# The head of a hybrid block: all tokens channels first, two blocks of u's product un-normed, the norm factor applied in the channel layout

## The chip, the cores and the metric

The kernel runs on one core of a Trainium2 chip. The metric is the device time of one execution in microseconds (us). The core has five engines that run side by side, each through its own instructions in order: TensorE (PE, with PEld for the loading of weights), VectorE (DVE), ScalarE (ACT), GpSimd (POOL) and SyncE (SP, which here only issues DMAs). An instruction waits until the engines and DMAs that make its inputs, or free its buffer, have signalled.

## The reference, cut to what matters

```python
def _mixer(xn, w_in, ...):
    proj = xn @ w_in                       # 1040 tokens x 1024 channels
    q, k, v, f_logit, u, gates = jnp.split(proj, SPLITS, axis=-1)
    y_a = _forgetting_attention(q, k, v, f_logit, b_forget) @ w_attn_out
    z = jax.nn.gelu(_s5(u, ...))           # 32 groups of 16 channels, 64 complex states each
    zg = z @ w_glu
    y_s = zg[..., :D_MODEL] * jax.nn.sigmoid(zg[..., D_MODEL:])
    g = jax.nn.sigmoid(gates)
    return (g[..., :D_MODEL] * y_a + g[..., D_MODEL:] * y_s) @ w_o

h = concatenate([meta, x])                 # 16 + 1024 tokens, 1024 channels
xn = _rmsnorm(h, norm_mix_g)               # h * rsqrt(mean(h*h) + eps) * g
h = h + _mixer(xn, ...)
h = h + _conv_ffn(_rmsnorm(h, norm_ffn_g), ...)
return _rmsnorm(h, norm_final_g)[N_META:]
```

Everything is float32. The norm factor of a token, `rsqrt(mean(h*h) + eps)`, is one number; a matrix product over channels may therefore be taken of `h * g` first and multiplied by the factor afterwards.

## The kernel before, in words

*Products.* A float32 operand is held as a pair, `hi` (rounded to what TensorE takes at speed) and `lo` (the rest), and each product is three matmuls: hi·hi, hi·lo, lo·hi. ACT makes `hi` by a cast, DVE makes `lo` by a subtraction (`split_lo`, L129).

*Layout.* TensorE contracts over the partitions, so the normed input is needed with channels on the partitions: the tiles `xhi` and `xlo`, 128 channels x 8 groups of channels x 1040 tokens. All projections read them.

*The head.* It makes `xhi` and `xlo` and computes u, 512 columns of the projection, in four blocks of tokens: block 0 has 272 (the 16 meta tokens and two tiles of 128), blocks 1 to 3 have 256 (two tiles each). A block's product is 4 groups of 128 columns (m = 0 to 3) x 8 groups of channels x 3 matmuls, 96 in all (`part`, L327 to L329).

- Block 0's tokens come channels first from DRAM (`x0t` into `xa`). ACT (L350) and DVE (L353) scale them by the norm's g and make the pair, without the norm factor. Their product enters four banks of PSUM (`first`) as the weights of u arrive. The factor is spread over the partitions: a DVE copy, a PE transpose (L370) and an ACT copy (L372) make `rsB`, and DVE multiplies the product by it on its way out of PSUM (L377).
- All other tokens, and block 0's once more, come as rows of 128 tokens (`xt`). ACT takes the sum of squares (L174), DVE and POOL make the factor (L176, L178: a power), DVE multiplies the rows by factor and g (L340), PE transposes them in eight pieces (L191), ACT and DVE make the pair (L193, L129). Block 0's tokens are made in this way last, behind block 3, since later products need them normed.
- ACT copies the products of blocks 1 to 3 out (L387). u is then written to DRAM by 32 DMAs (L394), those of m = 0 and 2 issued on SP, m = 1 and 3 on POOL, and is read back as `U` (L1724) in another layout for the SSM.

*Around the head.* The weights of the first gate columns are loaded behind the last row multiplication (L398, on POOL), cast by ACT (L399) and given their `lo` by ACT and an accumulating DMA (L135, L136). The SSM's tables are computed on DVE (L1456, L1459, with small copies on POOL, L1588 and L1589), and PE makes its kernel `Kt` (L1692) and its input map `Wi` (transposes L1713, copies on ACT L1714). The first SSM product is L1730, U with `Wi`. While these wait for data, PE works on the gate columns (L159 to L161). Later come q, k, v, the forget gate (L518, with weights `wf` made on POOL), the SSM's outputs, folded for a fast algorithm (`zf`, L559 on POOL; L584), attention, merge and the FFN.

*What sets the order.* A scheduler orders the instructions of each engine when the program is built, from a simulated timeline; `after(a, b)` adds an order by hand. The DMA loads of the head are chained on SP by `load` (L296), so that they arrive in the order written.

Of the kernel before, what the change touches and what calls it, by code (L numbers as in the profile page):

```python
# [9 lines left out]
F = mybir.dt.float32  # L10
# [3 lines left out]
AF = mybir.ActivationFunctionType  # L14
ALU = mybir.AluOpType
# [4 lines left out]
P = 128  # L20
# [27 lines left out]


@with_exitstack  # L50
def block_kernel(ctx, tc, x, meta, g1, x0t, g1t, w_q, w_k, w_v, w_f, w_u, w_g, b_f, w_ao, lam_d, bw_d, cw_d,
                 d_sk, l_dt, w_glu, w_o, g2, w_up, cwt_d, w_dn, gf, out, dbg=None, upto=99):
    nc = tc.nc
    dbg = dbg or {}
# [34 lines left out]
    def t_ps(name="tp"):  # L89
        return pp.tile([P, 512], F, tag="tp", name=name, bufs=2)  # L90
# [79 lines left out]
    def norm_factor(pl, src, n, bufs=10, sq=None):  # L170
        if sq is None:
            sq = pl.tile([P, D], BF, tag="sq", name="sq")
        ss = pl.tile([P, 1], F, tag="ss", name="ss", bufs=3)
        S.activation(sq[:n], src, AF.Square, accum_out=ss[:n])  # L174
        va = pl.tile([P, 1], F, tag="vr", name="vr", bufs=3)
        V.tensor_scalar(va[:n], ss[:n], 1.0 / D, EPS, ALU.mult, ALU.add)  # L176
        rs = pl.tile([P, 1], F, tag="rs", name="rs", bufs=bufs)
        GP.tensor_tensor(rs[:n], va[:n], nhalf[:n], ALU.pow)  # L178
        return rs
# [5 lines left out]
    def to_feature(xs, n, dhi, dlo, col, bank=st_ps):  # L185
        los = []
        for hf in range(2):
            tp = bank()
            t3 = tp.rearrange("p (k t) -> p k t", k=4)
            for k in range(4):  # L190
                PE.transpose(t3[:, k, :n], xs[:n, (4 * hf + k) * P:(4 * hf + k + 1) * P], ident[:n, :n])  # L191
            ho = dhi[:, 4 * hf:4 * hf + 4, col:col + n]
            S.copy(ho, t3[:, :, :n])  # L193
            los.append(split_lo(V, dlo[:, 4 * hf:4 * hf + 4, col:col + n], t3[:, :, :n], ho))
        return los
# [88 lines left out]
    uh = [wp.tile([P, 2, SW], R, tag=tag, name="uh") for tag in ("whi", "wlo") for _ in range(2)]  # L284
    xm = sp.tile([META, D], F, tag="tq", name="xm", bufs=3)

    xa = [sp.tile([P, 4, UN], F, tag="tq", name="xa", bufs=3) for _ in range(2)]
    g1T = n1.tile([P, KD], F, name="g1T")
    S.dma_start(g1T, g1t)
    S.dma_start(xm, meta)  # L290
    ssm_log, ssm_loads, ssm_steps = ssm(tc, after, sp, st_ps, ident, u_d, y_d, lam_d, bw_d, cw_d, d_sk, l_dt)
    queue = []

    def load(dst, src):

        queue.append(SY.dma_start(dst, src))  # L296
        if len(queue) > 1:
            after(*queue[:-3:-1])

    for j in range(4):  # L300
        load(xa[j // 2][:, 2 * (j % 2):2 * (j % 2) + 2], x0t[:, 2 * j:2 * j + 2])
        load(uraw[j], w_u[:, 2 * j:2 * j + 2])
    xts = [sp.tile([P, D], F, tag=tag, name="xt", bufs=n) for tag, n in (("Wi", 2), ("Gm", 2), ("sy", 3)) for _ in range(n)]
    g1B = xts.pop(4)
    g1_load = S.dma_start(g1B, g1.partition_broadcast(P))

    place = dict(zip((3, 4, 1, 2, 5, 6), xts))
    place[0] = xm

    def load_x(i):  # L310
        load(place[i], x[P * (i - 1):P * i])

    for i in range(1, 7):
# [11 lines left out]
    def part(ps, m, k, t, n):  # L325
        wh, wl = (w[k // 2][:, k % 2, P * m:P * m + P] for w in (uh, ul))
        PE.matmul(ps[:, :n], wh, xhi[:, k, t:t + n], start=(k == 0), stop=False)  # L327
        PE.matmul(ps[:, :n], wh, xlo[:, k, t:t + n], start=False, stop=False)
        PE.matmul(ps[:, :n], wl, xhi[:, k, t:t + n], start=False, stop=(k == KD - 1))  # L329

    def by_chunks(a):
        return a.rearrange("p (n j) -> p j n", j=CH)

    def factors(i):
        n = TILES[i][1]
        return norm_factor(n1, place[i][:n], n)

    def features(i, rs, behind=None):
        t, n = TILES[i]
        xn = V.scalar_tensor_tensor(out=place[i][:n], in0=place[i][:n], scalar=rs[:n], in1=g1B[:n],  # L340
                                    op0=ALU.mult, op1=ALU.mult)
        if behind is not None:
            after(xn, behind)
        return to_feature(place[i], n, xhi, xlo, t)[-1]

    first = [mm_ps() for _ in range(4)]
    for j in range(4):
        for k in (2 * j, 2 * j + 1):
            src, hi = xa[j // 2][:, k % 4], xhi[:, k, :UN]
            cp_ = S.activation(hi, src, AF.Copy, scale=g1T[:, k:k + 1])  # L350
            if k == 1:
                after(g1_load, cp_)
            V.scalar_tensor_tensor(out=xlo[:, k, :UN], in0=src, scalar=g1T[:, k:k + 1], in1=hi.bitcast(F),  # L353
                                   op0=ALU.mult, op1=ALU.subtract)
        S.copy(uh[j], uraw[j])
        split_lo(V, ul[j], uraw[j], uh[j])
        for m in range(4):
            for k in (2 * j, 2 * j + 1):
                part(first[m], m, k, 0, UN)
    for i in (7, 8):  # L360
        place[i] = sp.tile([P, D], F, tag="Tm", name="xt", bufs=2)
        load_x(i)

    rs0 = [factors(i) for i in range(3)]
    tp = t_ps()
    for i, rs in enumerate(rs0):
        t, n = TILES[i]
        rb = sp.tile([P, P], F, tag="wi", name="rb", bufs=2)
        V.tensor_copy(rb[:n], rs[:n].broadcast_to([n, P]))
        PE.transpose(tp[:, t:t + n], rb[:n], ident[:n, :n])  # L370
    rsB = sp.tile([P, UN], F, tag="wr", name="rsB", bufs=2)
    S.copy(rsB, tp[:, :UN])  # L372
    for i in (3, 4):
        ready = features(i, factors(i))
    n_log = len(ssm_log)
    for m in range(4):
        V.tensor_tensor(us[m][:, :, :UN // CH], by_chunks(first[m][:, :UN]), by_chunks(rsB), ALU.mult)  # L377

    for b, (t, n) in enumerate(UBLK[1:]):
        if b:  # L380
            for i in (3 + 2 * b, 4 + 2 * b):
                last = features(i, factors(i))
        for m in range(4):
            ps = mm_ps()
            for k in range(KD):
                part(ps, m, k, t, n)
            S.copy(us[m][:, :, t // CH:(t + n) // CH], by_chunks(ps[:, :n]))  # L387
# [1057 lines left out]
def ssm(tc, after, sp, s_ps, ident, u_d, y_d, lam_d, bw_d, cw_d, d_sk, l_dt):  # L1445
# [339 lines left out]
def _laid_out(x, meta_tokens, norm_mix_g, w_in, b_forget, w_attn_out, ssm_lambda_re, ssm_lambda_im, ssm_b_re, ssm_b_im,  # L1785
              ssm_c_re, ssm_c_im, ssm_d, ssm_log_dt, w_glu, w_o, norm_ffn_g, w_ffn_up, ffn_conv_w, ffn_conv_b,
              w_ffn_down, norm_final_g):
    import numpy as _np

    def by_rows(w):  # L1790

        return w.reshape(-1, P, w.shape[1]).transpose(1, 0, 2)

    def blocks(w):

        return w.reshape(w.shape[0] // P, P, -1, P).transpose(2, 1, 0, 3)
# [6 lines left out]
    x0 = _np.concatenate([meta_tokens, x[0]])[:UN]  # L1803
# [3 lines left out]
    return dict(x=x[0], meta=meta_tokens, g1=norm_mix_g[0], x0t=by_rows(x0.T), g1t=norm_mix_g[0].reshape(KD, P).T, w_q=blocks(q), w_k=blocks(k), w_v=by_rows(v),  # L1807
                w_f=by_rows(f), w_u=by_rows(u), w_g=blocks(g), b_f=b_forget[0], w_ao=blocks(w_attn_out[0]),
                lam=_np.concatenate([lam, lam]),
                bw=twice(ssm_b_re[0].transpose(1, 0, 2), ssm_b_im[0].transpose(1, 0, 2)),  # L1810
                cw=twice(ssm_c_re[0].transpose(2, 0, 1), ssm_c_im[0].transpose(2, 0, 1)),
                d_sk=ssm_d[0].reshape(G, GC).T, l_dt=ssm_log_dt[0], w_glu=blocks(w_glu[0]), w_o=w_o[0],
                g2=norm_ffn_g[0], w_up=blocks(w_ffn_up[0]), cwt=conv.reshape(4, -1, P).transpose(2, 0, 1),
                w_dn=w_ffn_down[0], gf=norm_final_g)
# [22 lines left out]
```

## Time and profile before

| what | value |
|---|---|
| time, median of 3 runs | 1486.72 us |
| lowest and highest run | 1483.04 and 1488.36 us |
| span of the profiled execution | 1485.7 us (the page gives no other time of it) |
| PE / PEld busy | 97% / 91% |
| DVE / ACT / POOL busy | 72% / 48% / 50% |
| mean DMA rate | 139 GB/s |

How to read the lines. A row of a stretch has its bounds and length in us, the busy time and count of PE, PEld, DVE, ACT and POOL, the clock granted to PE (1.00 is full), the DMA engines' busy share, and the GB/s. A row of a group has the line in the kernel, the engine, the operation, output and inputs, the shapes and the count; then the busy us, the mean ns of one, the idle time ahead and what ended it. A row of the timeline has start and length in us; in brackets stand the idle time ahead of it and what ended that. A row of waits has who waited for whom: us in total, times, the longest. SPq and POOLq are the queues on which DMAs are issued.

### The profile page before, as it was taken

How to read it: one execution, taken by the hardware profiler on the slowest of the kernel's cores; microseconds unless marked ns; L12 is line 12 of the kernel's file. 1: busy time of each engine (PE TensorE's matmuls, PEld its weight loads, DVE VectorE, ACT ScalarE, POOL GpSimd, SP SyncE). 2: the span in 40 equal slices, each digit the busy share in tenths (PEclk: the TensorE clock that was granted, in tenths of full speed). 3: DMA queues.
4: the chain of work that ended last, by engine and by line, in shares of the span. 5: the costliest groups of instructions: out<-in, count | busy, mean ns of one | idle time of the engine just before them, and what ended most of it. 6: DMA issues, size and time to landing. Idle time of an engine off the chain costs nothing. (4 is left out here: it accounts for less than half of the span.)

```text
span 1485.7 us, 26584 instructions
## 1 busy us (share of the span) xinstructions
PE 1440.4 (97%) x9712; PEld 1358.8 (91%) x9712; DVE 1071.4 (72%) x2173; ACT 712.2 (48%) x1384; POOL 742.1 (50%) x850
## 2 busy tenths in 40 slices
PE   7999997999999999999999999999999999998997
PEld 7989996998899999999888999999999999777886
DVE  6879648881566676647468987888877776788785
ACT  6434675541555665543546534444444445543433
POOL 1311125752456465524863144455544426789766
PEclk9999999999999999999999999999999999999999
DMA  6366571551127342047885135676653215765513
GB/s 246 86 157 157 128 163 50 177 160 43 48 79 178 93 111 90 26 148 256 257 158 185 57 109 141 178 199 188 174 143 100 84 57 180 286 203 148 168 40 114
DMA packets 91032, 206.72 MB, mean 139 GB/s; under 512 B 14651, under 2 KB 25531, under 8 KB 90517
## 3 DMA queue, kind: packets, MB, share of 16 engines
q1 hardware_dynamic: 69380, 159.73, 32.9%
q0 software_dynamic: 15296, 34.63, 13.2%
q10 hardware_dynamic: 6224, 10.65, 1.9%
q8 instruction: 77, 1.26, 0.3%
q14 instruction: 55, 0.44, 0.1%
HBM read 165.90 MB, written 69.35 MB: 158 GB/s over the span
## 5 line engine op out<-in xcount | busy, mean ns | idle before, releaser
L159 PE MATMUL mm<-xhi,whi 128*128 128x342 f32 (+2 forms) x488 | 159.4, 327 | 1.0 <-DVE q L129 1.0
L161 PE MATMUL mm<-xhi,wlo 128*128 128x342 f32 (+2 forms) x488 | 158.3, 325 | 0.0
L160 PE MATMUL mm<-xlo,whi 128*128 128x342 f32 (+2 forms) x488 | 157.7, 324 | 0.0
L1079 POOL TENSOR_TENSOR ov<-ov,og 128x1024 f32<-128x1024 f32 x21 | 51.1, 2434 | 125.6 <-ACT og L1078 121.7
L129 DVE TENSOR_TENSOR sw<-sf,sw 128x512 fp32r<-128x512 f32 x72 | 66.6, 925 | 50.0 <-ACT sw L1070 49.8
L1070 ACT CAST sw<-sf 128x512 fp32r<-128x512 f32 x72 | 44.9, 624 | 106.2 <-POOL sf L1196 74.5
L159 PEld LDWEIGHTS mm<-xhi,whi 128*128 128x128 f32 x488 | 91.9, 188 | 2.1 <-PE sp L714 0.8
L161 PEld LDWEIGHTS mm<-xhi,wlo 128*128 128x128 f32 x488 | 91.8, 188 | 0.3
L160 PEld LDWEIGHTS mm<-xlo,whi 128*128 128x128 f32 x488 | 91.9, 188 | 0.2
L763 ACT CAST th<-tp 128x256 fp32r<-128x256 f32 (+3 forms) x120 | 56.2, 472 | 62.5 <-PE tp L756 30.1
L129 DVE TENSOR_TENSOR tl<-tp,th 128x256 fp32r<-128x256 f32 (+3 forms) x120 | 65.2, 547 | 25.1 <-ACT th L763 23.7
L1196 POOL TENSOR_TENSOR sf<-raw,sf 128x512 f32<-128x512 f32 x36 | 59.1, 1641 | 44.8 <-DVE sw L129 44.7
L1196 POOL TENSOR_TENSOR sf<-raw 128x512 f32<-128x512 f32 x36 | 48.0, 1332 | 66.9 <-DMA raw<-in_w_up_dram 35.9
L221 PE MATMUL mm<-xhi,sw 128*128 128x258 f32 (+1 forms) x288 | 81.0, 281 | 0.0
L219 PE MATMUL mm<-xhi,sw 128*128 128x258 f32 (+1 forms) x288 | 80.8, 281 | 0.0
L220 PE MATMUL mm<-xlo,sw 128*128 128x258 f32 (+1 forms) x288 | 80.7, 280 | 0.0
L728 POOL TENSOR_SCALAR pt<-pt,nm 128x144 f32<-128x144 f32 (+4 forms) x72 | 51.8, 731 | 48.5 <-DVE nm L727 47.5
L1248 DVE SCALAR_TENSOR_TENSOR ov<-hv,cwt,ov 128x1024 f32<-128x1024 f32 x36 | 72.5, 2014 | 0.1
L1070 ACT CAST sw<-raw 128x512 fp32r<-128x512 f32 x70 | 43.0, 621 | 53.3 <-PE sp L221 25.5
L726 ACT ACTIVATE pt<-pt,nm 128x144 f32<-128x144 f32 (+4 forms) x72 | 52.9, 735 | 26.1 <-DVE nm L725 25.7
L719 DVE CUSTOM_DVE_ANT_0 pt<-sp,fb 128x328 f32<-128x328 f32 (+8 forms) x112 | 46.4, 430 | 20.0 <-PE sp L714 11.1
L756 PE MATMUL tp<-ident,pt 128*128 128x128 f32 (+1 forms) x360 | 58.3, 270 | 0.1
(708 smaller groups left out, 5702.1 us busy)
## 6 DMA issues: line engine op xcount, KB each, us to landing
raw<-in_w_up_dram SPq DMA_DIRECT2D x44, 512.0 KB, 3.6
t_d<-in_w_dn_dram POOLq DMA_DIRECT2D x44, 256.0 KB, 7.0
ar<-a_d SPq DMA_DIRECT2D x44, 256.0 KB, 5.1
wr<-t_d SPq DMA_DIRECT2D x44, 256.0 KB, 2.8
a_d<-ov SPq DMA_DIRECT2D x21, 512.0 KB, 2.6
wr<-in_w_dn_dram SPq DMA_DIRECT2D x33, 256.0 KB, 3.8
t_d<-in_w_dn_dram SPq DMA_DIRECT2D x22, 256.0 KB, 4.2
t_d<-t_d SPq DMA_DIRECT2D x22, 256.0 KB, 4.7
```

Of the source, the lines that this page charges most:

```text
L129: return eng.tensor_tensor(out_, src, hi.bitcast(F), ALU.subtract)
L159: yield PE.matmul(ps, whi[:, i, :], ahi[:, i], start=(i == 0), stop=False)
L160: yield PE.matmul(ps, whi[:, i, :], alo[:, i], start=False, stop=False)
L161: yield PE.matmul(ps, wlo[:, i, :], ahi[:, i], start=False, stop=(i == k - 1))
L219: PE.matmul(ps, a[0][:, i], bh, start=(i == 0 and not joins), stop=False, skip_group_check=True)
L220: PE.matmul(ps, a[0][:, i], bl, start=False, stop=False, skip_group_check=True)
L221: PE.matmul(ps, a[1][:, i], bh, start=False, stop=(i == kh - 1), skip_group_check=True)
L756: PE.transpose(tp[:kn, o:o + n], p_[:n, k0:k0 + kn], ident[:n, :n])
L763: S.copy(th[:kn, z:tw], tp[:kn, z:tw])
L1070: S.copy(hi, src)
L1196: sums.append(GP.tensor_tensor(f_, a, b, op))
L1248: V.scalar_tensor_tensor(out=o, in0=h_[:, j:SEQ + j], scalar=cwc(j, m), in1=o, op0=ALU.mult, op1=ALU.add)
```

## The change

The other tokens are loaded channels first as well (`xbt`, six more DMAs of 512 KB on SP); the rows are still loaded, but only for their sums of squares, and the row copy of g is no longer loaded. Block 1 enters u's product un-normed as block 0 does, and DVE multiplies its product by the factor on the way out. Block 0's product is copied out of PSUM by ACT, and POOL multiplies the copy by the factor afterwards. For every block the factor is spread over the partitions (`factors`). POOL then multiplies the channel tiles by it in place, and ACT and DVE make the normed pairs from them (`normed_features`): for blocks 2 and 3 ahead of their products, for blocks 0 and 1 for the later products. The transposes of the rows and the row multiplications go. Three small loads (the meta tokens, `l_dt`, `lam`) are issued on POOL's queue, not on ACT's.

In the order that the scheduler makes, POOL's queue has, one behind the other: the factors of the first tiles, block 0's four multiplications of u, block 0's channel tiles, block 1's, the remaining factors with the SSM's small copies, the issue of gate 0's load and of two more gate loads, then block 2's and block 3's channel tiles. ACT's queue has gate 0's cast ahead of the features of blocks 2 and 3. PE's queue has `Kt` ahead of the gate columns and 63 gate matmuls ahead of the first SSM product (before, some more). On SP, the second U is loaded behind the writes of `Tm` (before, right behind the first).

```diff
-    xa = [sp.tile([P, 4, UN], F, tag="tq", name="xa", bufs=3) for _ in range(2)]
+    xT = {0: [sp.tile([P, 4, UN], F, tag="tq", name="xa", bufs=3) for _ in range(2)]}
-    S.dma_start(xm, meta)
+    GP.dma_start(xm, meta)
...
-    g1_load = S.dma_start(g1B, g1.partition_broadcast(P))
...
+    def load_block(b, tag):
+        xT[b] = [sp.tile([P, 4, UBLK[b][1]], F, tag=tag, name="xT", bufs=2) for _ in range(2)]
+        for h_ in range(2):
+            load(xT[b][h_], xbt[b - 1, :, 4 * h_:4 * h_ + 4])
...
-    def features(i, rs, behind=None):
-        t, n = TILES[i]
-        xn = V.scalar_tensor_tensor(out=place[i][:n], in0=place[i][:n], scalar=rs[:n], in1=g1B[:n],
-                                    op0=ALU.mult, op1=ALU.mult)
-        if behind is not None:
-            after(xn, behind)
-        return to_feature(place[i], n, xhi, xlo, t)[-1]
+    def factors(b):
+        tp = t_ps()
+        t0, n_ = UBLK[b]
+        for i in TB[b]:
+            t, n = TILES[i]
+            rs = norm_factor(n1, place[i][:n], n)
+            rb = rbs[:n, i % 3]
+            V.tensor_copy(rb, rs[:n].broadcast_to([n, P]))
+            PE.transpose(tp[:, t - t0:t - t0 + n], rb, ident[:n, :n])
+        spread[b] = sp.tile([P, UN], F, tag=("wr", "wi")[b % 2], name="rsB", bufs=2)
+        S.copy(spread[b][:, :n_], tp[:, :n_])
+
+    def features(b, k):
+        t, n = UBLK[b]
+        src, hi = xT[b][k // 4][:, k % 4], xhi[:, k, t:t + n]
+        cp_ = S.activation(hi, src, AF.Copy, scale=g1T[:, k:k + 1])
+        cut = V.scalar_tensor_tensor(out=xlo[:, k, t:t + n], in0=src, scalar=g1T[:, k:k + 1], in1=hi.bitcast(F),
+                                     op0=ALU.mult, op1=ALU.subtract)
+        return cp_, cut
+
+    def normed_features(b):
+        t, n = UBLK[b]
+        for q in range(2):
+            GP.tensor_tensor(xT[b][q], xT[b][q], spread[b][:, :n].unsqueeze(1).broadcast_to([P, 4, n]), ALU.mult)
+        return [features(b, k)[1] for k in range(KD)][-1]
...
+    for m in range(4):
+        S.copy(us_part(0, m), by_chunks(first[m][:, :UN]))
+    ready = [features(1, k)[1] for k in range(KD)][-1]
+    factors(0)
     n_log = len(ssm_log)
+    factors(1)
     for m in range(4):
-        V.tensor_tensor(us[m][:, :, :UN // CH], by_chunks(first[m][:, :UN]), by_chunks(rsB), ALU.mult)
-    for b, (t, n) in enumerate(UBLK[1:]):
-        if b:
-            for i in (3 + 2 * b, 4 + 2 * b):
-                last = features(i, factors(i))
+        GP.tensor_tensor(us_part(0, m), us_part(0, m), by_chunks(spread[0]), ALU.mult)
+    for m in range(4):
+        ps = u_product(1, m)
+        V.tensor_tensor(us_part(1, m), by_chunks(ps[:, :UBLK[1][1]]), by_chunks(spread[1][:, :UBLK[1][1]]), ALU.mult)
+    for b in (2, 3):
+        factors(b)
+        normed_features(b)
+        if b == 3:
+            normed_features(0)
+            last = normed_features(1)
         for m in range(4):
-            ps = mm_ps()
-            for k in range(KD):
-                part(ps, m, k, t, n)
-            S.copy(us[m][:, :, t // CH:(t + n) // CH], by_chunks(ps[:, :n]))
-        if b == 2:
-            for i in range(3):
-                features(i, rs0[i], last)
+            ps = u_product(b, m)
+            S.copy(us_part(b, m), by_chunks(ps[:, :UBLK[b][1]]))
...
-    S.dma_start(ldt, l_dt.partition_broadcast(P))
+    GP.dma_start(ldt, l_dt.partition_broadcast(P))
-    S.dma_start(lam, lam_d)
+    GP.dma_start(lam, lam_d)
```

More of the change, by code (lines that the diff above doesn't have):

```diff
@@ L332, in by_chunks, with u_product, us_part @@
         return a.rearrange("p (n j) -> p j n", j=CH)
-    def factors(i):
-        n = TILES[i][1]
-        return norm_factor(n1, place[i][:n], n)
-    def features(i, rs, behind=None):
-        t, n = TILES[i]
-        xn = V.scalar_tensor_tensor(out=place[i][:n], in0=place[i][:n], scalar=rs[:n], in1=g1B[:n],
-                                    op0=ALU.mult, op1=ALU.mult)
-        if behind is not None:
-            after(xn, behind)
-        return to_feature(place[i], n, xhi, xlo, t)[-1]
+    TB = [(0, 1, 2), (3, 4), (5, 6), (7, 8)]
+    spread = {}
+    rbs = sp.tile([P, 3, P], F, tag="dt8", name="rb", bufs=1)
+    def factors(b):
[21 more added lines that the diff above has]
+        return [features(b, k)[1] for k in range(KD)][-1]
+    def u_product(b, m):
+        ps = mm_ps()
+        for k in range(KD):
+            part(ps, m, k, *UBLK[b])
+        return ps
+    def us_part(b, m):
+        t, n = UBLK[b]
+        return us[m][:, :, t // CH:(t + n) // CH]
     first = [mm_ps() for _ in range(4)]
@@ L348, in block_kernel @@
         for k in (2 * j, 2 * j + 1):
[L349 to L354, printed above, removed]
+            features(0, k)
         S.copy(uh[j], uraw[j])
@@ L359, in block_kernel @@
                 part(first[m], m, k, 0, UN)
+    load_block(2, "Tm")
+    for i in (5, 6):
+        load_x(i)
+    load_block(3, "Gm")
     for i in (7, 8):
-        place[i] = sp.tile([P, D], F, tag="Tm", name="xt", bufs=2)
         load_x(i)
[L364 to L374, printed above, removed]
+    for m in range(4):
+        S.copy(us_part(0, m), by_chunks(first[m][:, :UN]))
+    ready = [features(1, k)[1] for k in range(KD)][-1]
+    factors(0)
     n_log = len(ssm_log)
+    factors(1)
     for m in range(4):
-        V.tensor_tensor(us[m][:, :, :UN // CH], by_chunks(first[m][:, :UN]), by_chunks(rsB), ALU.mult)
-    for b, (t, n) in enumerate(UBLK[1:]):
-        if b:
-            for i in (3 + 2 * b, 4 + 2 * b):
-                last = features(i, factors(i))
-        for m in range(4):
-            ps = mm_ps()
-            for k in range(KD):
-                part(ps, m, k, t, n)
-            S.copy(us[m][:, :, t // CH:(t + n) // CH], by_chunks(ps[:, :n]))
-        if b == 2:
-            for i in range(3):
-                features(i, rs0[i], last)
+        GP.tensor_tensor(us_part(0, m), us_part(0, m), by_chunks(spread[0]), ALU.mult)
[8 more added lines that the diff above has]
+            last = normed_features(1)
+        for m in range(4):
+            ps = u_product(b, m)
+            S.copy(us_part(b, m), by_chunks(ps[:, :UBLK[b][1]]))
     for m in range(4):
@@ L1806, in _laid_out @@
     conv = _np.concatenate([ffn_conv_w[0], ffn_conv_b], axis=0)
[L1807 removed]
+    return dict(x=x[0], meta=meta_tokens, xbt=_np.stack([xT[:, :, t:t + n] for t, n in UBLK[1:]]),
+                x0t=xT[:, :, :UN], g1t=norm_mix_g[0].reshape(KD, P).T, w_q=blocks(q), w_k=blocks(k), w_v=by_rows(v),
                 w_f=by_rows(f), w_u=by_rows(u), w_g=blocks(g), b_f=b_forget[0], w_ao=blocks(w_attn_out[0]),
```

16 lines of the change are left out of this document (8 added, 8 removed).

## The prediction

> **What bounds the kernel now.** I read the page's busy shares and slices first, then the stretches of the head and of the stretch around 230 us, then PE's waits, then single rows. The page's own chain covers only the last instructions and says nothing of the head.
>
> ```profile
> span 1485.7 us, 26584 instructions
> PE 1440.4 (97%) x9712; PEld 1358.8 (91%) x9712; DVE 1071.4 (72%) x2173; ACT 712.2 (48%) x1384; POOL 742.1 (50%) x850
> PE   7999997999999999999999999999999999998997
> ```
>
> TensorE (PE) is busy 97% of the span; its first slice (37 us) is one of the few below 9. So whatever moves PE in the head moves the end, unless a later wait of PE takes it up. The stretches (PE, PEld, DVE, ACT, POOL busy, granted clock, DMA share, GB/s) and PE's waits up to 250 us:
>
> ```profile
> 20.00:25.00 5.00, 3.08 (x26) 2.84 (x25) 3.68 (x7) 3.48 (x8) 0.82 (x2) 1.00 1.02 410
> 30.00:35.00 5.00, 5.00 (x36) 5.00 (x35) 5.00 (x11) 1.18 (x2) 0.55 (x1) 0.77 0.01 2
> 92.80:100.00 7.20, 7.17 (x43) 6.81 (x44) 5.50 (x11) 4.45 (x12) 0.15 (x2) 0.76 0.27 76
> 220.00:230.00 10.00, 7.13 (x38) 6.78 (x38) 9.89 (x12) 6.31 (x11) 8.96 (x5) 0.84 0.05 19
> 230.00:240.00 10.00, 9.07 (x47) 7.18 (x45) 9.83 (x13) 5.76 (x13) 4.11 (x5) 0.82 0.18 52
> ```
> ```profile
> PE mm L518 <- POOL wf L129: 2.9, 1, 2.9
> PE sp L1730 <- ACT Wi L1714: 2.7, 1, 2.7
> ```
>
> PE waits in the head, is slowed after each wait (clock 0.77 and 0.76), waits once for U (L1730) and once for wf (L518, with the clock at 0.84 and 0.82 and DVE full beside it). POOL is nearly idle before 35 us.
>
> **The change, part by part.** Removed: 64 large PE transposes with their casts, and nine row multiplications on DVE.
>
> ```profile
> L191 PE MATMUL sp<-ident,xt 128*128 128x128 f32 x32 | 5.9, 314 | 4.8 <-DVE vr L176 3.1 <-DVE xlo L129 1.7
> L340 DVE SCALAR_TENSOR_TENSOR xt<-xt,rs 128x1024 f32<-128x1024 f32 x8 | 10.1, 1276 | 0.7 <-POOL rs L178 0.7
> L350 ACT ACTIVATE xhi<-xa,g1T 128x272 fp32r<-128x272 f32 x8 | 3.7, 512 | 1.1 <-DMA xa<-in_x0t_dram 1.0
> ```
>
> The sp half alone has 5.9 us of overlapping PE rows and 4.8 us of waits. DVE loses some 11.5 us of multiplications. In exchange ACT and DVE get 40 pairs like the third row, about 0.5 us each; they are spread over 60 us and each block's first pair is all that PE waits for, so I count 0.5 us a block. If that cover goes, a block's eight cost 4.
>
> Start and block 0. The meta tokens' square goes ahead of the first weight cast, a delay of 1.05; but the second pair of inputs comes by DMA anyway:
>
> ```profile
> 7.17 1.05 ACT L174 ACTIVATE sq<-xm 16x1024 bf16<-16x1024 f32 x1
> 11.12 0.93 ACT L350 ACTIVATE xhi<-xa,g1T 128x272 fp32r<-128x272 f32 x2 [1.04 <-DMA xa<-in_x0t_dram]
> 21.83 0.38 PE L370 MATMUL tp<-ident,rb 128*128 128x128 f32 x2
> 42.53 0.37 ACT L387 COPY usb<-po 128x256 f32<-128x256 f32 x1 [2.35 <-PE po L329]
> 67.94 0.28 PE L329 MATMUL po<-xhi,ul 128*128 128x256 f32 x1
> 68.65 0.28 PE L329 MATMUL po<-xhi,ul 128*128 128x256 f32 x1
> ```
>
> So block 0 ends near 22.3 instead of 21.83. Block 1 needs no norm now: the last two rows are two triples of matmuls apart, 0.355 a triple, so 32 triples are 11.36 and, with a few small transposes, block 1 ends near 34.1; before, its last copy came at 42.53. That is 8 us gained on PE.
>
> The loads: three more MB in channel layout, one of 0.5 MB gone; 2.5 MB at the 410 GB/s of the first stretch is 6.1 us more on SP's queue. They land by about 31, and POOL needs block 2's near 47, so nothing is charged. Were POOL quick, up to 6.1 would show. Three small DMAs move from ACT's queue to POOL's, idle there: nothing; at worst 1 us each on the SSM's tables.
>
> POOL is where the gain goes. It multiplies the copied u of block 0 (four of 128x8x34), block 0's channels (two of 128x1088), block 1's (two of 128x1024), and only then block 2's. The order of its queue puts those, the norm powers, the small SSM copies and the issue of gate 0's weights all ahead of block 2.
>
> ```profile
> L1079 POOL TENSOR_TENSOR ov<-ov,og 128x1024 f32<-128x1024 f32 x21 | 51.1, 2434 | 125.6 <-ACT og L1078 121.7 <-DVE ov L1109 3.9
> L600 POOL TENSOR_TENSOR cg<-cg,gl 128x342 f32<-128x342 f32 x24 | 22.8, 967 | 4.5 <-ACT cg L597 3.5 <-DMA gl<-g_d 1.0
> L559 POOL TENSOR_TENSOR zf<-zt 128x520 f32<-128x520 f32 x2 | 5.9, 2944 | 8.3 <-DMA zt<-y_d 8.3
> L178 POOL TENSOR_TENSOR rs<-vr,nhalf 128x1 f32<-128x1 f32 x8 | 5.3, 672 | 18.9 <-DVE vr L176 18.9
> 57.48 0.78 POOL L398 DMA_DIRECT2D g<-in_w_g_dram  x1
> 61.96 1.05 ACT L399 CAST g<-g 128x1024 fp32r<-128x1024 f32 x1 [4.81 <-DVE xt L340]
> 63.04 1.06 ACT L135 ACTIVATE g<-g 128x1024 fp32r<-128x1024 f32 x1
> 51.71 0.51 POOL L1588 COPY sm<-sm 128x32 f32<-128x32 f32 x3 [0.21 <-DVE sm L1456]
> ```
>
> Prices: 2.43 for 128x1024, in proportion 2.55 (estimate) for 1088. The u multiplication reads the factor with a stride of eight floats. Contiguous, two rows give (2434-967)/682 = 2.15 ns an element, hence 0.82 for 272; the strided row L559 gives 5.66 ns, hence 1.54. I take 1.5, because the stride is like L559's; ends 0.82 and 1.54. The Trainium skill, GPSIMD Engine Reference, section "7. Performance pitfalls for Q7 kernels", puts reads with a step above 8 bytes at half as much again, which speaks against this operand; by that rule the four would cost 1.23 each, an estimate, and the sum would be 1.1 lower. L559 is dearer than that rule.
>
> The powers of block 1 stand ahead in POOL's queue, and need ACT's squares behind the copies of block 0, so the u multiplications start near 25.4: block 0's end at 22.3, a copy of 0.37 and a square of 1.05 on ACT, a power of 0.67, and 1.0 for the hand-overs between engines (an estimate, after gaps such as the 0.7 of the L340 row). Then 4 x 1.5 = 6.0 to 31.4, 5.1 to 36.5, a power and 4.9 to 42.0, three powers (2.0) and fourteen small copies (2.4, by 0.51 for three) to 46.4. Here gate 0's load is issued. Its landing took 61.96 - 57.48 = 4.5, and ACT, in order, casts it (1.05 + 1.06) before it makes block 2's features: 46.4 + 4.5 + 2.0 = 52.9; POOL has block 2's first half by 50.7 (three DMA issues 1.9, one multiplication 2.4). With 0.5 for the first pair, PE starts block 2 at 53.4, 19.3 us after block 1. A wait brings the slow clock: at 0.77 over 5 us in the row above 1.2 is lost, more after a longer wait; I take 1.9 (ends 1.2 and 4). Blocks 2 and 3: 53.4 + 1.9 + 2 x 11.36 = 78.0.
>
> ```profile
> 73.53 0.58 PE L159 MATMUL mm<-xhi,g 128*128 128x342 f32 x2 [0.24 <-ACT xhi L193]
> 77.34 1.05 PE L1692 MATMUL sp<-Gm,sm 128*16 128x128 f32 x8
> 87.89 0.32 PE L159 MATMUL po<-xhi,whi 128*128 128x342 f32 x1
> 89.80 0.32 PE L159 MATMUL po<-xhi,whi 128*128 128x342 f32 x1
> 92.83 0.71 PE L1730 MATMUL sp<-U,Wi 128*128 128x130 f32 x4 [2.72 <-ACT Wi L1714]
> ```
>
> Before, PE went over to the gates at 73.53, after block 0's tokens were made again. After, nothing is left to be made: 78.0. **First term +4.5** (78.0 - 73.53; ends +1.1 with the cheap u price and the low clock loss, +8 with POOL a tenth dearer and the high one).
>
> U. Its data go out as writes of u, on SP one behind the other, and then come back:
>
> ```profile
> 64.01 0.63 ACT L387 COPY usb<-mm 128x256 f32<-128x256 f32 x2
> 64.39 14.65 SPq L394 DMA_DIRECT2D u_d<-usb  x16
> 79.14 1.18 SPq L1724 DMA_DIRECT2D U<-u_d  x2
> 92.19 0.59 ACT L1714 COPY Wi<-sp 128x512 f32<-128x512 f32 x1 [8.10 <-DMA U<-u_d]
> 80.00:84.00 4.00, 4.00 (x27) 4.00 (x26) 4.00 (x12) 1.89 (x3) 1.06 (x2) 1.00 1.08 217
> 88.00:92.00 4.00, 2.11 (x14) 1.83 (x12) 0.00 (x0) 0.00 (x0) 0.00 (x0) 1.00 1.04 312
> ```
>
> In the changed kernel the first column group of block 3 is done at 78.0 - 3 x 2.85 = 69.5, copied by 69.9; sixteen writes of 14.65 together end at 84.5, then U is issued. From issue to use it took 92.19 - 79.14 = 13.0; the second U went with it then and stands behind other loads now, which saves 0.5 MB at some 250 GB/s, 2.1. That is the late end, 95.4. The early end is 84.5 plus 0.5 MB at 410 GB/s, 1.3: 85.8. PE comes there at 78.0 + 1.9 (L1692) + 63 gate matmuls of 0.159 (twelve steps between the L159 rows are 1.91) + 0.9 = 90.8. So the wait is between 0 and 4.6 (7 with the second U's share put back). As much is on the DMA then as before, so I take 3.7, beside a clock loss like the old one of 0.24 x 7.2 = 1.7. **Second term: 3.7 - 2.7 = +1.0** (ends -4.4, no wait and no loss of clock, and +4.0).
>
> wf. In POOL's order it moves ahead of a multiplication and so comes earlier; its wait of 2.9 and some 2.9 of clock loss may go. But DVE stands at 9.89 and 9.83 of 10 there, so DVE's products are what is late next: only its 0.11 + 0.17 is left to gain. **Third term -0.3** (ends 0 and -5.8).
>
> Sum: 4.5 + 1.0 - 0.3 = +5.2 on a span of 1485.7. The profiled span is 1.0 below the median of the runs, 1486.7, and inside their spread, so I predict 1486.7 + 5.2 = 1491.9.
>
> **The rivals.** *U in time: no change.* U's wait is gone with its clock loss: 4.5 - 4.4 - 0.3 = -0.2, 1486.5. For it: U0 goes alone, and weights loaded at 58 to 64 before are fetched ten us ahead of the writes now. Against: a DMA share above 1 all through 80 to 92. It decides from a landing before 90.8.
>
> *Faster: wf decides.* The same with the wait at L518 and its slow clock really gone, which means that DVE's work there is not what PE needs next: 4.5 - 4.4 - 5.8 = -5.7, 1481.0; with POOL's contiguous price (2.7 less) 1478.3. It decides from 4.5 gained. For it: both stretches hold a clock of 0.82 to 0.84 and DVE comes lighter out of the head. Against: DVE full on both sides.
>
> *The change does nothing:* PE from 100 on absorbs any lateness in the waits near 230. Those waits hang on the same chain behind U, so I give it a part of the middle case alone.
>
> *By the clock rule.* The Trainium skill, TensorE: Matmul & The Clock Gate, section "What's actually happening", lets the clock fall only after some 3.4 us of idling; by that U's old wait of 2.7 should not have cost clock. The 0.76 row speaks against it. Had the loss another cause, it stays though U is in time: 4.5 - 2.7 - 0.3 = +1.5, 1488.2, still the middle case.
>
> **How the numbers follow.** No change, within 0.3% (4.5 us, about what this kernel's runs can tell): 0.30. Faster: 0.25. The forecast, slower: 0.45, own range 1488 to 1499. Two of ten left out at the ends of all cases: from 1480, just above the faster case's far end, to 1499 (+8 and +4.0 together are left out).
>
> **What would show it.** PE idle between about 34 and 53, released by ACT's features; POOL busy without a gap from 25; block 1's end near 34; gates from 78; a wait at the first product with U of some 3.7. Wrong if POOL's u multiplications take under 1 us, if block 2 begins before 48, or if PE gets U without waiting and the L518 wait is gone as well.

## The result, and the profile after

The changed kernel takes 1514.67 us (median of 4 runs, 1510.68 to 1515.74), the kernel before 1487.54 beside it: a ratio of 1.018, with a 95% interval of 1.0161 to 1.020. It is some 27 us slower, where 5.2 were predicted. The page of its profiled execution:

```profile
span 1513.8 us, 26522 instructions
PE 1434.2 (95%) x9646; PEld 1351.8 (89%) x9646; DVE 1091.4 (72%) x2192; ACT 721.1 (48%) x1409; POOL 765.6 (51%) x865
PE   6199998999999999999999999999999999998996
```

PE has 6.2 us less to do (1434.2 against 1440.4) and is idle for 79.6 us (1513.8 - 1434.2), against 45.3 before. The second slice shows where: 1 tenth busy. Up to the first product with U, PE is idle for 45.6 us (111.61 - 65.99), against 15.6 before (92.83 - 77.22); that is 30.0 of the 34.3. That stretch as a whole and two parts of it, first of the kernel before, then of the changed one:

```profile
0.00:92.83 92.83, 77.22 (x568) 74.64 (x568) 67.91 (x221) 42.01 (x75) 26.09 (x60) 0.96 0.61 182
40.00:60.00 20.00, 19.47 (x165) 19.03 (x164) 16.95 (x85) 5.19 (x12) 6.70 (x20) 1.00 0.05 10
60.00:80.00 20.00, 18.09 (x144) 16.89 (x143) 15.81 (x36) 10.71 (x19) 10.86 (x20) 1.00 0.88 220
```
```profile
0.00:111.61 111.61, 65.99 (x478) 63.48 (x479) 88.35 (x248) 50.99 (x100) 51.68 (x75) 0.83 0.54 170
40.00:60.00 20.00, 0.92 (x2) 0.36 (x2) 19.95 (x58) 3.33 (x9) 14.39 (x23) 0.50 0.23 79
60.00:80.00 20.00, 10.20 (x57) 9.53 (x58) 19.96 (x48) 9.13 (x20) 7.76 (x6) 0.59 0.17 27
```

Between 40 and 80 us PE does 11 us of work, partly at half clock; DVE (the third busy time) is busy without a gap, and POOL is not. PE's waits of the changed kernel up to 300 us, the longest but for the first weights, which both kernels wait for:

```profile
PE tp L351 <- DVE vr L176: 13.8, 1, 13.8
PE tp L351 <- DVE rb L350: 11.5, 2, 6.5
...
PE mm L332 <- DVE xlo L360: 6.6, 1, 6.6
PE mm L331 <- ACT xhi L359: 2.9, 1, 2.9
PE sp L1755 <- DMA U<-u_d: 2.7, 1, 2.7
```

Four of the five are in the head, 34.8 us together, and DVE ends 31.9 of these: PE's transposes that spread the norm factor (L351) wait for DVE's `vr` and `rb`, the products of block 2 (L332) for DVE's `lo` parts. Rows of PE, DVE, POOL and ACT in that stretch, with others between them left out:

```profile
33.82 0.28 PE L333 MATMUL po<-xhi,ul 128*128 128x256 f32 x1
63.87 1.01 PE L331 MATMUL mm<-xhi,uh 128*128 128x256 f32 x3 [2.89 <-ACT xhi L359]
71.68 0.58 PE L332 MATMUL mm<-xlo,uh 128*128 128x256 f32 x1 [6.59 <-DVE xlo L360]
111.61 0.68 PE L1755 MATMUL sp<-U,Wi 128*128 128x130 f32 x4 [2.73 <-DMA U<-u_d]
```
```profile
27.73 6.02 DVE L1478 TENSOR_SCALAR sm<-sm 128x32 f32<-128x32 f32 x1
54.33 5.42 DVE L360 SCALAR_TENSOR_TENSOR xlo<-xT,g1T,xhi 128x256 fp32r<-128x256 f32 x1
59.96 0.35 DVE L350 COPY rb<-rs 128x128 f32<-128x128 f32 x2
64.12 2.85 DVE L1481 TENSOR_TENSOR bt<-bw,sm 128x512 f32<-128x512 f32 x1
71.15 0.87 DVE L360 SCALAR_TENSOR_TENSOR xlo<-xT,g1T,xhi 128x256 fp32r<-128x256 f32 x2
```
```profile
25.00 3.69 POOL L403 TENSOR_TENSOR usb<-usb,rsB 128x272 f32<-128x272 f32 x4
28.66 5.04 POOL L367 TENSOR_TENSOR xa<-xa,rsB 128x1088 f32<-128x1088 f32 x2
36.61 0.59 POOL L178 TENSOR_TENSOR rs<-vr,nhalf 128x1 f32<-128x1 f32 x1 [2.90 <-DVE vr L176]
53.13 0.61 POOL L423 DMA_DIRECT2D g<-in_w_g_dram  x1 [1.35 <-DVE sm L1481]
54.80 4.65 POOL L367 TENSOR_TENSOR xT<-xT,rsB 128x1024 f32<-128x1024 f32 x2
61.46 4.96 POOL L367 TENSOR_TENSOR xT<-xT,rsB 128x1024 f32<-128x1024 f32 x2 [2.01 <-ACT rsB L353]
```
```profile
61.01 0.37 ACT L353 COPY rsB<-tp 128x256 f32<-128x256 f32 x1 [6.78 <-PE tp L351]
61.28 1.05 ACT L424 CAST g<-g 128x1024 fp32r<-128x1024 f32 x1
```

One operation of DVE on 128x32, 0.17 us long elsewhere, lasts 6.02 us: it starts with the last multiplication of u and ends as POOL's pair of multiplications on `xa` ends, at 33.7, so three POOL instructions went by. One `lo` operation lasts 5.42 and ends at 59.7, just behind POOL's pair on `xT`, at 59.5. One product of 128x512 lasts 2.85; it starts beside the last pair and ends 0.55 us behind it, at 66.97. The same two kinds of DVE operations over the whole stretch from 18 to 82 us, and that product, show how far they are lengthened: first the changed kernel, then one with the same instructions where the twelve large multiplications do not run on POOL (the first experiment below):

```profile
L360 DVE SCALAR_TENSOR_TENSOR xlo<-xT,g1T,xhi 128x256 fp32r<-128x256 f32 x28 | 17.2, 654 | 0.0
L1478 DVE TENSOR_SCALAR sm<-sm 128x32 f32<-128x32 f32 x20 | 9.8, 510 | 0.1
...
L1481 DVE TENSOR_TENSOR bt<-bw,sm 128x512 f32<-128x512 f32 x2 | 3.5, 1764 | 0.0
```
```profile
L360 DVE SCALAR_TENSOR_TENSOR xlo<-xT,g1T,xhi 128x256 fp32r<-128x256 f32 x28 | 12.1, 468 | 0.0
...
L1478 DVE TENSOR_SCALAR sm<-sm 128x32 f32<-128x32 f32 x20 | 3.1, 174 | 0.1
...
L1481 DVE TENSOR_TENSOR bt<-bw,sm 128x512 f32<-128x512 f32 x2 | 1.4, 682 | 0.0
```

In these three groups alone DVE is held for 13.9 us: 5.1 + 6.7 + 2.1. DVE then comes late to the factors and the `lo` parts, which stand behind the SSM's tables in its queue.

### The profile page after: what moved, and what is told of

It is laid out like the page before. It is cut to its first block, busy times and chain, and to the rows that moved or that the text cites. A ratio compares the mean times of both kernels' runs of the same rounds, so it can differ in the third digit from the quotient of the medians.

```text
span 1513.8 us, 26522 instructions
## 1 busy us (share of the span) xinstructions
PE 1434.2 (95%) x9646; PEld 1351.8 (89%) x9646; DVE 1091.4 (72%) x2192; ACT 721.1 (48%) x1409; POOL 765.6 (51%) x865
## 5 line engine op out<-in xcount | busy, mean ns | idle before, releaser
L129 DVE TENSOR_TENSOR sw<-sf,sw 128x512 fp32r<-128x512 f32 x72 | 71.1, 988 | 51.9 <-ACT sw L1095 51.9
L744 DVE CUSTOM_DVE_ANT_0 pt<-sp,fb 128x328 f32<-128x328 f32 (+8 forms) x112 | 46.4, 430 | 20.0 <-PE sp L739 11.8
L129 DVE TENSOR_TENSOR sw<-raw,sw 128x512 fp32r<-128x512 f32 x70 | 54.5, 782 | 5.9 <-ACT sw L1095 5.5
```

Source lines behind the costliest of these rows:

```text
L129: return eng.tensor_tensor(out_, src, hi.bitcast(F), ALU.subtract)
```

## The experiments

Three theories were set against each other. A is the prediction's: POOL's own queue holds block 2 back. B: DVE stands still while POOL multiplies. C: the order of DVE's queue, which has block 2's factors and `lo` parts behind the SSM's tables, does it. Ratios are to the kernel before on the same chip (medians of 1489.2 to 1490.6 there); the changed kernel stands at 1.018.

| run | edit | ratio, 95% interval |
|---|---|---|
| e1 | all twelve multiplications on DVE | 0.9961 (0.9946 to 0.9976) |
| e2 | channel multiplications cut thin | 1.0032 (1.0015 to 1.005) |
| e3 | SSM's tables later | 1.0028 (1.0015 to 1.0041) |
| e4 | blocks 0 and 1 last on POOL | 1.0148 (1.0132 to 1.0164) |
| e5 | before, with idle POOL work, two inputs | 1.0052 (1.0037 to 1.0067) |
| e6 | before, with idle POOL work, one input | 1.0069 (1.005 to 1.0088) |
| e7 | e1 and e3 together | 0.997 (0.9958 to 0.9983) |
| e8 | e7, and block 2 first on DVE | 1.0041 (1.0027 to 1.0055) |
| e9 | blocks 0 and 1 on DVE | 1.0099 (1.0076 to 1.0122) |
| e10 | blocks 2 and 3 on DVE | 1.0118 (1.0101 to 1.0135) |
| e11 | u's four on DVE | 1.0142 (1.0127 to 1.0157) |
| e12 | the three small loads back on ACT | 1.0175 (1.0156 to 1.0195) |

**e1, the multiplications on DVE.**

```diff
-            GP.tensor_tensor(xT[b][q], xT[b][q], spread[b][:, :n].unsqueeze(1).broadcast_to([P, 4, n]), ALU.mult)
+            V.tensor_tensor(xT[b][q], xT[b][q], spread[b][:, :n].unsqueeze(1).broadcast_to([P, 4, n]), ALU.mult)
...
-        GP.tensor_tensor(us_part(0, m), us_part(0, m), by_chunks(spread[0]), ALU.mult)
+        V.tensor_tensor(us_part(0, m), us_part(0, m), by_chunks(spread[0]), ALU.mult)
```

> The changed kernel, with its twelve large POOL multiplications (four of u, eight of channel tiles) issued on DVE instead. Theory A, POOL's own queue is what holds block 2 back (the prediction's mechanism): block 2 is released some 6 us earlier but DVE gets about 12 us more, so between no change and +6, 1514 to 1520 us. Theory B, DVE stands still while POOL multiplies (its rows between 25 and 67 us are about 21 us longer than the same rows elsewhere): DVE loses 21 and gains 12, so about 9 us or more faster, 1500 to 1506. Theory C, only the order of DVE's queue counts (factors and lo parts of block 2 behind the SSM's tables): 12 us more work in the same queue, 1522 to 1528.

1485.51 us: 33 us less than the changed kernel by the ratios ((1.018 - 0.9961) x 1489), and faster than the kernel before. That is more than B had said and the opposite of C. Of PE's 34.8 us of waits this one is left, and 1.5 for `xhi`:

```profile
PE tp L351 <- DVE rb L350: 9.4, 2, 5.1
```

DVE was given some 12 us of work (4 x 0.68 + 2 x 1.27 + 6 x 1.21) and lost its 14 and more of standing still, as the two fences of groups above show. The scheduler also put DVE's queue into another order here, so this run alone does not part B from C.

**e2, thin multiplications; e3, tables later; e4, blocks 0 and 1 late.** In e2 the output lacks the norm factor on all but 8 tokens of each block.

```diff
-            GP.tensor_tensor(xT[b][q], xT[b][q], spread[b][:, :n].unsqueeze(1).broadcast_to([P, 4, n]), ALU.mult)
+            GP.tensor_tensor(xT[b][q][:, :, :8], xT[b][q][:, :, :8], spread[b][:, :8].unsqueeze(1).broadcast_to([P, 4, 8]), ALU.mult)
```

> The changed kernel, with each of the eight POOL multiplications of channel tiles cut to 8 columns per channel group, so the norm factor is left out of the rest; all waits stay. Theory A: 19 us of POOL's queue go, block 2 no longer waits for POOL and is released about 6 us earlier by it, then by gate 0's cast: 1503 to 1508. Theory B: DVE loses some 17 fewer us to POOL, block 2's products start near 54 instead of 71.7: 1495 to 1499. Theory C: DVE's queue has the same work as before, so 1510 to 1514.

1494.49 us, 22 us less than the changed kernel, about as B had said. It is not as fast as e1, though it has less work: block 2 starts at 42.9, but then PE waits for U:

```profile
PE sp L1755 <- DMA U<-u_d: 6.2, 1, 6.2
```

In e3 a hand-written order holds the SSM's tables until block 2's normed pairs; POOL's work stays.

```diff
-        normed_features(b)
+        last_b = normed_features(b)
+        if b == 2:
+            ready = last_b
```

> The changed kernel, with one order by hand changed: the SSM's tables on DVE may start behind block 2's normed pairs, not behind block 1's un-normed ones. Theory A: no change, 1512 to 1516. Theory B alone: the same 21 us are lost on DVE, at another place; block 2's lo parts come some 10 us earlier, the tables as much later, 1504 to 1516. Theory C: block 2 starts near 55 instead of 71.7 and the SSM product waits for its tables instead, 1500 to 1508.

1493.26 us, 23 us less, and more than C had said; A had said no change. All twelve multiplications are still on POOL, and DVE is still held by them, but now at the places where it has little to do. POOL's multiplications of block 2 start at 46.18 instead of 54.80, though the same ones stand ahead of them: what has gone are POOL's waits for DVE and the small copies for the tables between them. A stretch and rows of POOL, DVE and PE:

```profile
20.00:40.00 20.00, 14.55 (x123) 14.34 (x121) 11.01 (x20) 13.85 (x33) 16.27 (x13) 0.91 0.70 257
```
```profile
46.18 9.27 POOL L367 TENSOR_TENSOR xT<-xT,rsB 128x1024 f32<-128x1024 f32 x4
```
```profile
32.34 5.36 DVE L360 SCALAR_TENSOR_TENSOR xlo<-xa,g1T,xhi 128x272 fp32r<-128x272 f32 x4
...
51.39 7.12 DVE L360 SCALAR_TENSOR_TENSOR xlo<-xT,g1T,xhi 128x256 fp32r<-128x256 f32 x8 [5.46 <-ACT xhi L359]
```
```profile
55.80 0.58 PE L332 MATMUL mm<-xlo,uh 128*128 128x256 f32 x1 [3.16 <-DVE xlo L360]
```

POOL is busy for 16.27 of these 20 us and DVE for 11.01, against 19.28 in the changed kernel; the eight `lo` parts of block 2 take 7.12 where eight free ones are 3.7 (468 ns each). PE has block 2 under way at 55.8, not at 71.7. Here and in most of the runs below the scheduler moved other instructions too, on POOL as well as on DVE.

In e4 the two blocks that PE needs last come last on POOL.

```diff
+            if behind is not None:
+                after(mu, behind)
...
-            normed_features(0)
-            last = normed_features(1)
+            normed_features(0, last3)
+            last = normed_features(1, last3)
```

> The changed kernel, with POOL's multiplications of blocks 0 and 1 ordered behind block 3's. Theory A: 9.7 us of multiplications leave POOL's queue ahead of block 2, so block 2 starts about 10 us earlier: 1501 to 1505. Theory B: DVE's 21 us of standing still move, about 10 of them behind block 2: 1503 to 1508. Theory C: block 2's factors still stand behind the tables in DVE's queue, less than 4 us gained: 1510 to 1515.

1513.18 us, 5 us less than the changed kernel by the ratios. POOL's queue was relieved of 9.7 us ahead of block 2, and block 2 did start early, at 44.4 instead of 63.87. A's 1501 to 1505 are missed all the same, because the time was lost again behind it. The holding went with the multiplications to where the `lo` parts of the later blocks stand, and PE waited for them. And gate 0's load, which waits for block 1's pairs, was issued at 99.21 instead of 53.13, so that PE waited for its cast as well:

```profile
L360 DVE SCALAR_TENSOR_TENSOR xlo<-xT,g1T,xhi 128x256 fp32r<-128x256 f32 x20 | 16.6, 902 | 3.1 <-ACT xhi L359 3.1
```
```profile
PE mm L332 <- DVE xlo L360: 8.0, 5, 2.2
PE mm L159 <- ACT g L426: 4.3, 1, 4.3
```

So this run does not decide against A by itself. e1 and e3 do: e1 came out 33 us faster where A had said none to 6 slower, and e3 gained 23 where A had said none.

**e5 and e6, idle POOL work in the kernel before.** Neither touches the norm or the loads of the kernel before; POOL only gets work that nobody needs. The order of DVE's queue in the head is that of before in e6 but for one row multiplication; in e5 some rows of tables and `lo` parts moved as well.

```diff
+    pad = uraw[0].rearrange("p a n -> p (a n)")
+    for _ in range(8):                                   # e5
+        after(GP.tensor_tensor(pad, pad, pad, ALU.mult), ready)
+    for _ in range(18):                                  # e6, in place of the eight
+        after(GP.tensor_scalar(pad, pad, 1.0, 0.0, ALU.mult, ALU.add), ready)
```

> The kernel before, with eight idle multiplications of 128x1024 by itself on POOL (two inputs, 19.5 us in all), between 25 and 55 us, where POOL has little to do and DVE is full; its output is unchanged. Theory A, only POOL's queue counts: the factors of the last tiles stand behind some of them, 0 to 4 us slower than before. Theory B, DVE stands still while POOL multiplies: DVE's rows in that stretch grow by 10 to 19 us in all, and the kernel is 5 to 12 us slower than before.

> The kernel before, with eighteen idle POOL operations of one input and a constant on 128x1024 (19.4 us in all) at the same place; its output is unchanged. Theory A: as the run with two inputs, 0 to 4 us slower than before. Theory B, if two tensor inputs are what holds DVE up: DVE's rows keep their length, 0 to 4 us slower, and at least 4 us faster than the run with two inputs. Theory B, if any large POOL operation holds DVE up: as the run with two inputs.

1497.99 and 1500.10 us: 0.52% and 0.69% slower, 8 and 10 us. PE waits for DVE's `lo` parts (L328) for 8.8 and 10.1 us, where it was 0.3 before. The work has one input or two, the loss is much the same, so it does not take two inputs on POOL. DVE and POOL rows of e6, then of e5:

```profile
37.51 1.02 DVE L1456 TENSOR_SCALAR sm<-sm 128x32 f32<-128x32 f32 x1
38.68 1.03 DVE L1456 TENSOR_SCALAR sm<-sm 128x32 int32<-128x32 f32 x1
```
```profile
35.33 11.30 POOL L377 TENSOR_SCALAR uraw<-uraw 128x1024 f32<-128x1024 f32 x9
```
```profile
37.95 1.27 DVE L340 SCALAR_TENSOR_TENSOR xt<-xt,rs 128x1024 f32<-128x1024 f32 x1
39.15 1.87 DVE L1456 TENSOR_SCALAR sm<-sm 128x32 f32<-128x32 f32 x1
```
```profile
36.04 9.94 POOL L377 TENSOR_TENSOR uraw<-uraw 128x1024 f32<-128x1024 f32 x4
```

A DVE operation of 0.17 us takes 1.02 beside POOL operations of 1.04 each, and 1.87 beside those of 1.89: it lasts until the POOL instruction beside it ends. Then one or two of DVE's get in before POOL's next: the 1.27 in e5 is the operation's own length, and POOL's four take 9.94 us, not 4 x 1.89 = 7.6. In these two runs the engines take turns by whole instructions; in the changed kernel, as shown above, one DVE instruction stood through two or three of POOL's. The idle work also stood ahead of two norm factors in POOL's own queue, and no run takes that part of the 8 to 10 us away; the lengths of DVE's rows do not depend on it.

**e7 and e8, the two cures together.** e7 has the edits of e1 and e3. e8 has besides the order of e4, with the multiplications on DVE.

> The changed kernel with both edits that were tried one by one: the twelve multiplications on DVE, and the SSM's tables behind block 2's normed pairs. If DVE's standing still and its order are two causes that add up: PE's remaining waits for the factors (9.4 us with the multiplications on DVE) shrink to some 4, 1478 to 1483 us. If they are one cause (with nothing standing still the order is harmless): as with the multiplications alone, 1484 to 1487; and if the tables then come late for the SSM's first product, slower than that, 1488 to 1494.

> As the run before, and besides the multiplications of blocks 0 and 1 ordered behind block 3's pairs, so that block 2 stands first in DVE's queue. If DVE's queue is what holds block 2 back: PE's idle time between block 1 and block 2 falls below 5 us, 1474 to 1480 us unless the SSM's tables or the normed blocks 0 and 1 come late for the gates. Theory A, POOL's queue: nothing of it is left there, as the multiplications on DVE alone, 1484 to 1487.

e7 takes 1485.69 us, as e1 does (their intervals overlap): the two gains of 33 and 23 us do not add up. Both act on the same lateness: DVE's queue is too long in front of block 2, because of what holds it and because of what stands in it. With the holding taken away the order no longer matters (e7 against e1); with the order changed the holding still costs some 8 us (1.0028 in e3 against 0.997 in e7). e8 takes 1496.63 and misses its expectation by 17 us. Block 2 does start early, at 38.3, but PE then waits for what was put behind it:

```profile
PE po L159 <- ACT whi L146: 10.6, 1, 10.6
...
PE sp L1742 <- DVE Vm L1485: 3.9, 2, 2.1
```

As in e4, the edit also moved gate 0's load: it was issued at 81.70, in e1 at 42.88. With the holding gone, neither change of order gained anything: e7 is as fast as e1, and e8 only has others wait.

**e9 to e12, the parts.** The channel multiplications of blocks 0 and 1 alone, those of blocks 2 and 3 alone, and those of u alone went to DVE; in e12 only the three small loads went back.

```diff
-            GP.tensor_tensor(xT[b][q], xT[b][q], ...
+            (V if b < 2 else GP).tensor_tensor(xT[b][q], xT[b][q], ...      # e9
+            (V if b > 1 else GP).tensor_tensor(xT[b][q], xT[b][q], ...      # e10
...
-        GP.tensor_tensor(us_part(0, m), us_part(0, m), ...
+        V.tensor_tensor(us_part(0, m), us_part(0, m), ...                   # e11
...
-    GP.dma_start(xm, meta)
+    S.dma_start(xm, meta)                                                   # e12, and l_dt and lam likewise
```

> The changed kernel with only the channel multiplications of blocks 0 and 1 on DVE (u's four, and blocks 2 and 3, stay on POOL). If DVE's standing still counts by its length: it loses some 10 us fewer between 28 and 42 us and gains 4.8 of work, so 4 to 8 us faster than the changed kernel, 1506 to 1510. If it counts only where block 2's factors and pairs are in the queue (54 to 67 us): no change, 1512 to 1516.

> The changed kernel with only the channel multiplications of blocks 2 and 3 on DVE, in nearly the same order of DVE's queue. If DVE's standing still counts by its length: it loses some 9 us fewer between 54 and 67 us and gains 4.7 of work, 4 to 8 us faster than the changed kernel, 1506 to 1510. If it counts only where block 2's pairs are in the queue: 8 to 14 us faster, 1500 to 1506, and most of the gain of all twelve is here. If the order is all: 3 to 5 us slower, 1517 to 1520.

> The changed kernel with only the four multiplications of u's block 0 on DVE. They took 3.7 us on POOL and held DVE for about 1.5; on DVE they are 2.5 us of work: no change, 1512 to 1517. The prediction's price for them, 1.5 us each on POOL, was too high, and if they were what POOL's queue turned on, 3 to 4 us faster, 1510.

> The changed kernel with the three small loads (meta tokens, l_dt, lam) back on ACT's queue. By the prediction's price of nothing: 1512 to 1517. If the tables' start hangs on them, up to 3 us either way.

e9: 1502.77 us, e10: 1506.68, e11: 1510.71. By the ratios that is 12, 9 and 6 us less than the changed kernel, 27 together of e1's 33, each with some 4 us either way: every part of the holding costs something, and none of them carries it all. That holds for this order of DVE's queue; e3 shows that where the holding falls matters too. e10 is the cleanest of these runs for B: DVE's queue is that of the changed kernel up to the first multiplication that was moved, and it gets 4.7 us more work. Still it is faster, with the held `lo` parts back at their length and block 2 starting without the wait of 6.59. Behind that multiplication some `lo` parts now stand ahead of the last tables, and what this is worth was not tried:

```profile
L360 DVE SCALAR_TENSOR_TENSOR xlo<-xT,g1T,xhi 128x256 fp32r<-128x256 f32 x29 | 12.9, 478 | 0.0
```
```profile
57.32 1.01 PE L331 MATMUL mm<-xhi,uh 128*128 128x256 f32 x3 [3.01 <-ACT xhi L359]
```

e9 and e11 were better than expected; in both the scheduler moved DVE's queue as well, and how much of their 12 and 6 us is order was not tried. e12, 1.0175 against 1.018, is no change.

## Why the prediction was wrong

Its direction was right; its size was not, and neither was its reason.

- *Start, block 0, block 1.* Right. The last matmul of block 1 ends at 34.1 (33.82 + 0.28), the predicted 34.1.
- *Loads, small loads.* Right: nothing in PE's waits ends with them, and e12 is no change.
- *POOL's prices.* The channel multiplications were right (5.04 and 4.65 a pair, predicted 5.1 and 4.9). u's were 0.92 each, not 1.5: the strided row L559 was the wrong neighbour, and the contiguous end, 0.82, nearly right; under 1 us was one of the prediction's own signs of being wrong. By the prediction's own sum this alone takes off 2.3 us, 4 x (1.5 - 0.92). By the GPSIMD Engine Reference of the Trainium skill, section "7. Performance pitfalls for Q7 kernels", the estimate had been 1.23; at 0.92 this operand shows less of its penalty than that. (In proportion 1088 columns are 2.59, not 2.55; nothing hangs on it.)
- *"POOL is where the gain goes".* This is the step that failed. It laid POOL's instructions end to end, let nothing else be late, and had PE begin block 2 at 53.4; PE began at 63.87 and got on at 71.68. POOL was not busy without a gap. It was ahead of that schedule at 33.7 (predicted 36.5) and behind it at the issue of gate 0's weights, 53.1 against 46.4, since it had waited for DVE's `vr` and for the SSM's small operations. ACT came to gate 0's cast at 61.28, not because the weights were late but because the copy of `rsB` ahead of it waited, over PE's transpose, for `rb` on DVE. In the place of POOL's own queue the runs showed DVE's: runs that made it shorter in front of block 2, or less held, gained 9 to 33 us (e1, e2, e3, e9, e10), and e3 did so with all of POOL's multiplications left.
- *"DVE loses some 11.5 us of multiplications".* Taken as a relief, and DVE's queue was not walked through. It took 40 `lo` parts of 0.47 us instead, where 16 of 0.69 went with the transposes; the tables started at 19 us, not at 31, and stood ahead of the factors of blocks 2 and 3. The cover of "0.5 us a block" for the pairs was not there: from block 2's first matmuls at 63.87 to those with `lo` at 71.68 passed 7.8 us.
- *What was missing altogether:* that POOL's work takes time from DVE. The Trainium skill, GPSIMD Engine Reference, section "8. Key points", says that POOL shares its SBUF interfaces with VectorE, with contention for DVE instructions that read two tensors from SBUF or run in a mode that uses two ports. The runs agree for the contention and give its size, which the section does not: a DVE instruction is held to the end of the POOL instruction beside it (1.02 us for 0.17 in e6), or of the two or three that follow one another (6.02 for 0.17 in the changed kernel). The trace of before held a hint, 4.62 us for a POOL operation of 128x256 at 221 us beside a full DVE, where the mean of its kind is 0.99; the prediction did not use it.
- *First term.* u's product ended at 96.4, predicted 78.0: +22.8 at this place, not +4.5. The clock loss was as predicted: 0.213 us a matmul instead of 0.118 from 71.7 to 76.5, some 2.1 us.
- *Second term.* The wait for U was 2.73 as before (2.72), where 3.7 was predicted; it came at 111.61 instead of 92.83. The clock loss behind it, 1.7 us before and taken as the same, was not there: the granted clock was 1.00 from 111.6 to 118.8. So the term was -1.7, not +1.0. Two waits of the same length, one with a slow clock behind it and one without: what decides that, and with it the rival by the clock rule, stays open.
- *Third term.* The wait at the forget gate's product is gone, and PE waits for DVE's `kl` there (2.6 and 0.7, against 2.9), as the prediction had said of what is late next.
- *How 22.8 became 28.* The product with U came 18.8 us later (111.61 - 92.83): PE had idled 30.0 us more and had done 11.2 us less (65.99 against 77.22). Of these 11.2, 6.2 are gone for good and 5.0 were done later. With 4.3 us more of idle time behind U, that makes the 28.1 us between the spans.
- *Left over.* Near the end of the kernel PE waits longer for `hs` in the changed kernel than in e1, by 2.4 us in the row below and by some 4 with its neighbours, with the same instructions. The first row is of the changed kernel, the second of e1. Nothing was tried on this.

```profile
PE tp L1390 <- DVE hs L1400: 5.1, 2, 4.4
```
```profile
PE tp L1390 <- DVE hs L1400: 2.7, 2, 2.0
```

Of the rivals, none came true in its time. That the forecast's range ended at 1499 came from pricing each engine's queue by its own rows and giving the ends to POOL alone.

## What to carry to other kernels

Work given to POOL is not free for DVE: beside large POOL operations a small DVE operation can last as long as one of them, or as several back to back, so a multiplication that takes 2.4 us on POOL and 1.2 on DVE is dearer on POOL when DVE's queue is what others wait for. When a change moves work between engines, walk through the queue of every engine that feeds the critical one, in the new order, not only the queue that gets the work. If the order is free, let POOL's large operations fall where DVE is idle (e3), or keep them off it (e1, which is faster than both kernels).

## What the runs showed of the hardware that was not expected

DVE and POOL shut each other out by whole instructions. In e5 and e6 they took turns, one or two of DVE between two of POOL: DVE operations of 0.17 us on 128x32 lasted 1.02 us beside POOL operations of 1.04, and 1.87 beside those of 1.89, with one tensor input on either side as well as with two. Where POOL's multiplications followed one another without a gap, DVE did not always get its turn: in the changed kernel one operation of 0.17 us lasted 6.02, through three of them, and a `lo` part of 0.47 lasted 5.42, through two. POOL is held in turn, 9.94 us for four operations that take 1.89 each when nothing holds them.

Held were operations of DVE with a scalar (`TENSOR_SCALAR`), with a scalar and a tensor, and with two tensors, all from SBUF. Operations with one of two inputs from PSUM were not held: `usb<-mm,rsB` took 0.61 us beside a multiplication of 2.34 (changed kernel, at 37.34), `xlo<-tp,xhi` 0.67 beside one of e5 (at 36.17). Nor does all work of POOL hold all of DVE's: in e5 four operations with a scalar and a tensor took 0.19 us each beside a `MEMSET` of 0.98 (at 46.06).

And u's multiplication with a factor read at a stride of eight floats took 0.92 us on POOL, 0.10 more than the prediction's estimate for a contiguous one.
